# One gate matrix in eight moved to ScalarE, gain rows of the expert layers' end loaded sooner, lead tiles in two banks

## The chip, the cores and the metric

The kernel runs on one core of a Trainium2 chip. A core has TensorE (PE in the profile, with its weight loads as PEld), VectorE (DVE), ScalarE (ACT), GpSimd (POOL) and SyncE (SP), which here only issues transfers; each engine works through its own list of instructions in order. The metric is the device time of one execution in microseconds (us).

## The reference, cut to what matters

Two blocks stand behind each other, each with a mixer (retention and pooling; then a gated recurrence and a state-space scan) and an expert layer. The change touches the two expert layers alone. 512 tokens each pick 128 of 16384 experts, eight heads with 16 each:

```python
s1, i1 = lax.top_k(s[:, :, 0], PEER_TOPK)
s2, i2 = lax.top_k(s[:, :, 1], PEER_TOPK)
cand = s1[..., :, None] + s2[..., None, :]
cidx = i1[..., :, None] * PEER_NKEYS + i2[..., None, :]
best, pos = lax.top_k(cand, PEER_TOPK)
eidx = jnp.take_along_axis(cidx, pos, axis=-1)
g = jax.nn.softmax(best, axis=-1)
act = jax.nn.gelu(jnp.einsum('thkd,td->thk', u[eidx], hb), approximate=False)
out = jnp.einsum('thk,thkd->td', g * act, v[eidx])
```

Behind it stand x = x + g2 * out and a norm with a gain row.

## The kernel before

The class `Peer` does an expert layer, once for each block ("layer 1" and "layer 2" below). For 384 of the 512 tokens it does not gather rows but multiplies with all 16384 experts, 128 at a time (a "tile"), and weights each product with a dense matrix G[expert, token] that holds the gates; the last 128 tokens go the gathering way (`sparse`), between the dense work.

**The gate stage** (end of `early`) builds G. A token's 128 choices are pairs (first, second) of numbers below 128, with a gate each. For eight tokens at a time (an "octet", 48 of them in a layer) `onehots` makes, on DVE, `gb`: 1 where a lane's second number equals the column (one instruction for all eight tokens, L2070), and for each token `ga`: the gate where its first number equals the column, else 0 (eight instructions, L2074). `gbuild` multiplies ga and gb of each token on PE, four tokens to a PSUM bank named `ch` (three such banks), and ACT copies each bank to the staging tile `gst` (L2088), which SP stores when 32 tokens are in it (L2090). `ga` and `gb` have three buffers each; the loop makes octet n+2 before it multiplies octet n. The lists of first, second and gate come from `lists_T`, which transposes them into `hkT`.

Between the octets PE does the products of the first 60 expert tiles with the tokens (`s_quarters`, tiles `mm`): a quarter of a tile per octet, so that four octets ("a cycle") go with one tile: one split of a loaded tile `ur` into high and low parts (`uh` on ACT, L111, `ul` on DVE, L114) and one Gelu (`act`, L2113).

**The lead** (`steady`, first loop) does five more tiles with `s_step`, all in the PSUM bank `p0` (L2254), before the loop over the 128 tiles of the second matrix begins. `s_step` issues a load three tiles ahead, splits the next tile, and then multiplies its own.

**The loop** over i takes each tile's G and activation, loads a tile of `v` two ahead (`vr`, L2275), prepares it (`v_prep`: G times activation, then high and low parts `vh`, `vl`, `wh`, `wl`), and multiplies into eight banks `pv`. `side` slips the gathered rows of the sparse tokens in between. When the 256 gathered rows are done, `ending` calls `done` (in `ffn`), which loads two rows across all partitions: the layer's output gate (`gr<-gate`, L2356) and the gain of the norm (L2357). Then it updates the sparse tokens (`take`, L2368; `update`, L2376 and L2378) in halves between the last tiles.

Of the kernel before, what the change touches and what calls it, by code (L numbers as in the profile page):

```python
# [10 lines left out]
F32 = mybir.dt.float32  # L11
# [4 lines left out]
AF = mybir.ActivationFunctionType  # L16
ALU = mybir.AluOpType
# [1746 lines left out]
class Peer:  # L1764
# [73 lines left out]
    def early(self):  # L1838
        tc, E, P, ps = self.tc, self.E, self.pfx, self.ps
        W0, *pools = self.prev  # L1840
        kp = tc.alloc_tile_pool(name=P + "k", bufs=2, side="right")
# [18 lines left out]
        self.acts = tc.alloc_tile_pool(name=P + "a", bufs=6)  # L1860
        qp = tc.alloc_tile_pool(name=P + "q", bufs=2)
        ws = Weights(E, qp, [(self.wq, 128 * j, 128) for j in range(2, 16)], 2, (self.WLO,))
        self.hkT = kp.tile([128, self.ND, 3, 128], F32, name="hkT", bufs=1)
        self.gf = kp.tile([128, 4, 8, 16], F32, name="gf", bufs=1)
        self.ef = kp.tile([128, 4, 8, 16], F32, name="ef", bufs=1)
        self.at = 1
# [27 lines left out]
        nc, v = self.nc, self.nc.vector  # L1894
# [160 lines left out]
    def lists_T(self, tb, i12):  # L2055
        nc, E = self.nc, self.E
        pt = self.ps.tile([128, 3, 128], F32, name="tp")
        nc.tensor.transpose(pt[:, 0, :], i12[:, 0, :], E.ident)
        nc.tensor.transpose(pt[:, 1, :], i12[:, 1, :], E.ident)
        nc.tensor.transpose(pt[:, 2, :], self.gf[:, tb].rearrange("p h k -> p (h k)"), E.ident)  # L2060
        nc.scalar.activation(self.hkT[:, tb], pt, AF.Copy)

    def onehots(self, n, gp):

        nc, E = self.nc, self.E
        tb, q = divmod(n, 16)
        sh = [128, 8, 128]
        a = gp.tile(sh, F32, name="ga")
        b = gp.tile(sh, F32, name="gb")
        nc.vector.tensor_tensor(b, E.iota[:, None, :].to_broadcast(sh),  # L2070
                                self.hkT[:, tb, 1, q * 8:q * 8 + 8, None].to_broadcast(sh), op=ALU.is_equal)
        for i in range(8):
            first, gate = (self.hkT[:, tb, z, q * 8 + i:q * 8 + i + 1] for z in (0, 2))
            nc.vector.tensor_scalar(a[:, i, :], E.iota, first, gate, op0=ALU.is_equal, op1=ALU.mult)  # L2074
        return a, b

# [70 lines left out]
    def steady(self, vp, psv):  # L2147
        E = self.E
        self.accs = vp.tile([128, 1024], F32, name="accs", bufs=1)
        sps = self.sparse(vp)  # L2150
        next(sps)
        self.pv = [[psv.tile([128, 512], F32, name=f"pv{tb}{dh}") for dh in range(2)] for tb in range(self.ND)]
        done = 0
        for _ in range(self.LEAD):
            self.s_step(self.L0 + done)
            if not done:
                self.v_load(0, vp)
                self.v_load(1, vp)
            done += 1
        self.v_prep(0, vp)  # L2160
        if self.fill is not None:
            E.fill, E.rate = self.fill(vp), 0.4
        owed = 0.0
        full = self.s_by[-1] - self.LEAD + self.S_END + self.VF * (self.SPARSE_END - self.S_END)
        finish = None

        def rows(tail=False):
            return vp.tile([128, 1024], F32, name="vr" if tail else "gr", bufs=3 if tail else self.LAG + 1)

        def ending():  # L2170
            nonlocal finish
            yield from sps
            finish = take, update, squares, factor = self.done(rows)
            src = self.accs[:, :512], self.accs[:, 512:]
            for h in range(2):
                yield
                take(3, src, h)
                update(3, h)
            for h in range(2):
                yield  # L2180
                squares(3, h)
            yield
            factor(3)

        steps = ending()

        def side():
            nonlocal owed
            owed += 256 / full * (1.0 if i < self.S_END else self.VF)
            while owed >= 1 and finish is None:  # L2190
                owed -= 1
                next(steps)
            if finish is not None:
                next(steps, None)

        for i in range(124):
            self.v_load(i + 2 if i < 122 else 128, vp)
            if i == 117 and self.after is not None:
                self.after.preload()
            if i == 119:  # L2200
                self.v_load(124, vp, True)
                self.v_load(125, vp, True)
            elif i in (122, 123):
                self.v_load(i + 4, vp)
            while done < self.s_by[i]:
                self.s_step(self.L0 + done, side)
                done += 1
                E.tick()
            side()
            if i < 123:  # L2210
                self.v_prep(i + 1, vp)
            if i in (121, 122):
                self.v_prep(i + 3, vp, True)
            elif i == 123:
                self.v_prep(126, vp)
            E.tick()
            self.v_mm((i,))
        self.v_prep(127, vp)
        self.acts.release()
        after = self.after  # L2220
        if after is not None:
            after.open()
        E.drain()
        for _ in steps:
            pass
        self.v_mm(range(124, 128))
        take, update, squares, factor = finish

        def add(tb, h):
            update(tb, h)  # L2230
            squares(tb, h)

        later = []
        for tb in range(self.ND):
            for h in range(2):
                if tb == 0 and after is not None:
                    after.weights()
                take(tb, self.pv[tb], h)
                if (tb, h) == (2, 0):
                    factor(1)  # L2240
                if tb == 2 and after is not None:
                    later.append(lambda h=h: add(2, h))
                else:
                    add(tb, h)
                if (tb, h) == (1, 1):
                    factor(0)
        if after is not None:
            after.tail = *later, lambda: factor(2)
        else:
            factor(2)  # L2250

    def s_step(self, e, side=None):
        self.s_load(e + 3)
        pm = self.E.pair.tile([128, self.TD], F32, name="p0")  # L2254
        self.s_split(e + 1, "dve")
        if side:
            side()
        self.s_mm(e, pm, range(8))
        self.s_gelu(e, pm)
# [211 lines left out]
```

## Time and profile before

| | us |
|---|---|
| median of 3 runs | 3571.43 (3567.28 to 3572.85) |
| the profiled execution, own time | 3559.23 |
| its span, first to last instruction | 3557.5 |
| PE busy | 3377.0 (95%) |
| DVE busy | 2827.5 (79%) |
| ACT busy | 1358.8 (38%) |

The shares are means over stages with different limits; the gate stages, from about 911 to 1080 us and from 2542 to 2712 us, and the ends of the expert layers, about 1835 to 1925 us and 3465 to 3557 us, are read by themselves. In a row of the timeline, the number behind an arrow in brackets is the idle time of the engine just before, and what ended it.

### The profile page before, as it was taken

How to read it: one execution, taken by the hardware profiler on the slowest of the kernel's cores; microseconds unless marked ns; L12 is line 12 of the kernel's file. 1: busy time of each engine (PE TensorE's matmuls, PEld its weight loads, DVE VectorE, ACT ScalarE, POOL GpSimd, SP SyncE). 2: the span in 40 equal slices, each digit the busy share in tenths (PEclk: the TensorE clock that was granted, in tenths of full speed). 3: DMA queues.
4: the chain of work that ended last, by engine and by line, in shares of the span. 5: the costliest groups of instructions: out<-in, count | busy, mean ns of one | idle time of the engine just before them, and what ended most of it. 6: DMA issues, size and time to landing. Idle time of an engine off the chain costs nothing.

```text
span 3557.5 us, 50422 instructions
## 1 busy us (share of the span) xinstructions
PE 3377.0 (95%) x18339; PEld 3003.5 (84%) x18339; DVE 2827.5 (79%) x5892; ACT 1358.8 (38%) x1930; POOL 981.1 (28%) x848
## 2 busy tenths in 40 slices
PE   8989889999999999999998898999998999999998
PEld 5878668999888888888886787899987888888886
DVE  6655766898996888888876685788996888888886
ACT  4223324333673333333334324432574333333333
POOL 3212531000002444444431442000000444454440
PEclk9999999999999999999999999999999999999999
DMA  5451664443458999999993222344457999999995
GB/s 193 131 160 57 189 208 122 136 142 127 175 199 323 364 376 344 364 346 363 351 317 101 71 72 91 103 139 141 144 195 261 357 373 356 359 351 347 365 331 188
DMA packets 418745, 830.18 MB, mean 233 GB/s; under 512 B 37948, under 2 KB 249776, under 8 KB 415424
## 3 DMA queue, kind: packets, MB, share of 16 engines
q1 hardware_dynamic: 344320, 558.41, 46.3%
q0 software_dynamic: 74176, 268.55, 20.4%
q8 instruction: 144, 2.36, 0.3%
q14 instruction: 105, 0.86, 0.1%
HBM read 744.52 MB, written 82.33 MB: 232 GB/s over the span
## 4 chain that ended last, share of the span: by engine, by line
PE 72%; DVE 18%; DMA 5%; issue 2%; ACT 2%; SPq 1%; POOL 0%; DVEq 0%; ACTq 0%; POOLq 0%
PE pv L118 9%; PE pv L119 9%; PE pv L120 9%; PE mm L118 8%; PE mm L120 8%; PE mm L119 8%; DVE ga L2074 5%; PE p L120 5%; PE p L118 5%; PE p L119 5%; DVE gb L2070 3%; DMA ada<-in_ada_w_dram 2%; DVE ul L114 1%; DMA ur<-in_peer_u_tiles_dram 1%; DMA x<-in_ada_w_dram 1%
## 5 line engine op out<-in xcount | busy, mean ns | idle before, releaser
L2321 POOL DMA_INDIRECT gr<-in_peer_u_dram,rb x256 | 338.7, 1323 | 1455.0 <-DMA ur<-in_peer_u_tiles_dram 1020.4
L118 PE MATMUL pv<-vh,wh 128*128 128x512 f32 x1512 | 591.1, 391 | 23.6 <-ACT wh L2295 23.6
L119 PE MATMUL pv<-vl,wh 128*128 128x512 f32 x1512 | 590.8, 391 | 0.7 <-DVE vl L2296 0.7
L120 PE MATMUL pv<-vh,wl 128*128 128x512 f32 x1512 | 590.5, 391 | 0.0
L2296 DVE TENSOR_TENSOR vl<-vr,vh 128x1024 fp32r<-128x1024 f32 x252 | 308.6, 1224 | 215.9 <-ACT vh L2294 209.1
L2321 POOL DMA_INDIRECT gr<-in_peer_v_dram,rb x256 | 344.6, 1346 | 389.8 <-DVE accs L2342 331.5
L114 DVE TENSOR_TENSOR ul<-ur,uh 128x1024 fp32r<-128x1024 f32 x256 | 312.7, 1221 | 108.5 <-ACT uh L111 108.4
L118 PE MATMUL p<-hi,uh 128*128 128x384 f32 x1088 | 367.3, 338 | 9.7 <-ACT act L2113 9.7
L120 PE MATMUL p<-hi,ul 128*128 128x384 f32 x1088 | 366.8, 337 | 0.5 <-DVE ul L114 0.5
L2294 ACT ACTIVATE vh<-vr 128x1024 fp32r<-128x1024 f32 x252 | 266.1, 1056 | 264.2 <-issue 224.8
L119 PE MATMUL p<-lo,uh 128*128 128x384 f32 x1088 | 366.3, 337 | 0.0
L118 PEld LDWEIGHTS pv<-vh,wh 128*128 128x128 f32 x1512 | 284.8, 188 | 82.3 <-ACT wh L2295 26.0
L118 PE MATMUL mm<-hi,uh 128*128 128x384 f32 x960 | 334.9, 349 | 3.6 <-ACT qT L1871 3.6
L120 PEld LDWEIGHTS pv<-vh,wl 128*128 128x128 f32 x1512 | 284.4, 188 | 60.7 <-DVE wl L2297 1.5
L2113 ACT ACTIVATE act<-p 128x384 f32<-128x384 f32 x136 | 66.9, 492 | 700.1 <-PE p L120 684.3
L119 PEld LDWEIGHTS pv<-vl,wh 128*128 128x128 f32 x1512 | 284.7, 188 | 57.2 <-DVE vl L2296 2.5
L2342 DVE SCALAR_TENSOR_TENSOR accs<-gr,rb,accs 128x1024 f32<-128x1024 f32 x254 | 325.7, 1282 | 5.4 <-DMA gr<-in_peer_v_dram,rb 0.7
L120 PE MATMUL mm<-hi,ul 128*128 128x384 f32 x960 | 324.5, 338 | 3.9 <-DVE ul L114 3.9
L119 PE MATMUL mm<-lo,uh 128*128 128x384 f32 x960 | 323.7, 337 | 0.0
L2337 DVE SCALAR_TENSOR_TENSOR gr<-gr,hs 128x1024 f32<-128x1024 f32 x256 | 302.9, 1220 | 2.0 <-DMA gr<-in_peer_u_dram,rb 2.0
L111 ACT ACTIVATE uh<-ur 128x1024 fp32r<-128x1024 f32 x256 | 269.0, 1051 | 18.9 <-DMA ur<-in_peer_u_tiles_dram 15.2
L118 PE MATMUL mm<-hi,whi 128*128 128x512 f32 (+1 forms) x656 | 262.7, 400 | 2.8 <-ACT whi L111 1.9
(634 smaller groups left out, 7199.6 us busy)
## 6 DMA issues: line engine op xcount, KB each, us to landing
ur<-in_peer_u_tiles_dram SPq DMA_DIRECT2D x256, 512.0 KB
vr<-in_peer_v_dram SPq DMA_DIRECT2D x252, 512.0 KB
raw<-in_w_in_dram SPq DMA_DIRECT2D x60, 512.0 KB
ada<-in_ada_w_dram SPq DMA_DIRECT2D x96, 256.0 KB
fG<-gst SPq DMA_DIRECT2D x12, 2048.0 KB
f_2G<-gst SPq DMA_DIRECT2D x12, 2048.0 KB
x<-in_ada_w_dram SPq DMA_DIRECT2D x64, 256.0 KB
raw<-in_peer_wq_dram SPq DMA_DIRECT2D x32, 512.0 KB
```

What stands on the lines that cost most here:

```text
L111: nc.scalar.activation(hi, src, AF.Copy)
L114: (nc.vector if e_lo == "dve" else nc.gpsimd).tensor_tensor(lo, src, hi.bitcast(F32), op=ALU.subtract)
L118: nc.tensor.matmul(out, a_hi, b_hi, start=start, stop=False)
L119: nc.tensor.matmul(out, a_hi, b_lo, start=False, stop=False)
L120: nc.tensor.matmul(out, a_lo, b_hi, start=False, stop=stop)
L2070: nc.vector.tensor_tensor(b, E.iota[:, None, :].to_broadcast(sh), self.hkT[:, tb, 1, q * 8:q * 8 + 8, None].to_broadcast(sh), op=ALU.is_equal)
L2074: nc.vector.tensor_scalar(a[:, i, :], E.iota, first, gate, op0=ALU.is_equal, op1=ALU.mult)
L2294: nc.scalar.activation(vh, raw, AF.Copy)
L2296: nc.vector.tensor_tensor(vl, raw, vh.bitcast(F32), op=ALU.subtract)
L2321: nc.gpsimd.indirect_dma_start(out=r, out_offset=None, in_=self.u if n < 128 else self.v, in_offset=bass.IndirectOffsetOnAxis(ap=self.eidx ...
L2337: nc.vector.scalar_tensor_tensor(r, r, 1.0, self.hs, op0=ALU.mult, op1=ALU.mult, accum_out=dots[:, j:j + 1])
L2342: nc.vector.scalar_tensor_tensor(accs, r, w[:, j:j + 1], accs, op0=ALU.mult, op1=ALU.add)
```

## The change

One ga in eight, that of an octet's last token, is made by two instructions on ACT: the distance |first - column|, then max(0, gate - gate * distance), which is the gate at distance 0 and 0 from distance 1 on. For it `hkT` has a fourth list, minus the gate, which DVE makes in `lists_T`. `done` is called behind gathered row 253, two rows sooner, and nothing else of `ending` moves. The five lead tiles take the banks p0 and p1 in turn.

```diff
-        self.hkT = kp.tile([128, self.ND, 3, 128], F32, name="hkT", bufs=1)
+        self.hkT = kp.tile([128, self.ND, 4, 128], F32, name="hkT", bufs=1)
...
-        nc.scalar.activation(self.hkT[:, tb], pt, AF.Copy)
+        nc.scalar.activation(self.hkT[:, tb, 0:3], pt, AF.Copy)
+        nc.vector.tensor_scalar(self.hkT[:, tb, 3], self.hkT[:, tb, 2], -1.0, None, op0=ALU.mult)
...
-            first, gate = (self.hkT[:, tb, z, q * 8 + i:q * 8 + i + 1] for z in (0, 2))
+            first, gate, less = (self.hkT[:, tb, z, q * 8 + i:q * 8 + i + 1] for z in (0, 2, 3))
+            if i == 7:
+
+                nc.scalar.activation(a[:, i, :], E.iota, AF.Abs, scale=-1.0, bias=first)
+                nc.scalar.activation(a[:, i, :], a[:, i, :], AF.Relu, scale=less, bias=gate)
+                continue
             nc.vector.tensor_scalar(a[:, i, :], E.iota, first, gate, op0=ALU.is_equal, op1=ALU.mult)
...
-            yield from sps
-            finish = take, update, squares, factor = self.done(rows)
+            for n, _ in enumerate(sps):
+                if n == 253:
+                    made = self.done(rows)
+                yield
+            finish = take, update, squares, factor = made
...
-        pm = self.E.pair.tile([128, self.TD], F32, name="p0")
+        first = e - self.L0 < self.LEAD
+        pm = self.E.pair.tile([128, self.TD], F32, name=f"p{(e - self.L0) % 2 if first else 0}")
```

On ACT, a cycle of the gate stage of layer 1 before is one Gelu, one split and eight copies of banks:

```order
L2113 ACTIVATE act<-mm 128x384
L2088 ACTIVATE gst<-ch 128x4x128 x2
L111 ACTIVATE uh<-ur 128x1024
L2088 ACTIVATE gst<-ch 128x4x128 x6
L2113 ACTIVATE act<-mm 128x384
```

The same cycle on ACT now:

```order
L2119 ACTIVATE act<-mm 128x384
L2077 ACTIVATE ga<-iota,hkT 128x128
L2078 ACTIVATE ga<-ga,hkT 128x128
L2094 ACTIVATE gst<-ch 128x4x128 x2
L111 ACTIVATE uh<-ur 128x1024
L2077 ACTIVATE ga<-iota,hkT 128x128
L2078 ACTIVATE ga<-ga,hkT 128x128
L2094 ACTIVATE gst<-ch 128x4x128 x2
L2077 ACTIVATE ga<-iota,hkT 128x128
L2078 ACTIVATE ga<-ga,hkT 128x128
L2094 ACTIVATE gst<-ch 128x4x128 x2
```

Behind these rows a fourth pair and its two copies end the cycle. Each pair stands ahead of the copies of the octet two before its own. No table load is added on ACT. On DVE the octets have seven ga each, and three small instructions stand ahead of the first octet:

```order
L114 TENSOR_TENSOR ul<-ur,uh 128x1024
L2062 TENSOR_SCALAR hkT<-hkT 128x128 x3
L2071 TENSOR_TENSOR gb<-iota,hkT 128x1024
L2080 TENSOR_SCALAR ga<-iota,hkT 128x128 x7
L2071 TENSOR_TENSOR gb<-iota,hkT 128x1024
```

Before, a row "ga x8" stood in place of each "ga x7", and no row of L2062. On SP, the transfers of layer 1's end stand before in this order (`hi<-in_w_in_dram` are weights of the next mixer):

```order
L2275 DMA vr<-in_peer_v_dram 128x1024 x4
L152 DMA hi_16768<-in_w_in_dram 128x4x256
L152 DMA hi_16769<-in_w_in_dram 128x4x256
L152 DMA hi_16770<-in_w_in_dram 128x4x256
L152 DMA hi_16771<-in_w_in_dram 128x4x256
L2268 DMA Go<-fG 128x12x128
L2271 DMA old<-fA 128x1536
L2275 DMA vr<-in_peer_v_dram 128x1024 x2
L2268 DMA Go<-fG 128x12x128
L2271 DMA old<-fA 128x1536
L2275 DMA ur<-in_peer_v_dram 128x1024 x2
L2356 DMA gr<-gate_78 128x1024
```

And now:

```order
L2285 DMA vr<-in_peer_v_dram 128x1024 x2
L2366 DMA gr<-gate_78 128x1024
L2367 DMA lo_16761<-in_final_g_dram 128x1024
L2285 DMA vr<-in_peer_v_dram 128x1024 x2
L152 DMA hi_16825<-in_w_in_dram 128x4x256
```

The two rows of the layer's end move ahead of fourteen other transfers of that stretch; layer 2 has the same move, without the four `hi` loads. On ACT, the rows of the lead show the banks (a Gelu reads each tile from its bank), before:

```order
L2113 ACTIVATE act_10250<-p0_10223 128x384
L111 ACTIVATE uh_10163<-ur_10161 128x1024
L2113 ACTIVATE act_10291<-p0_10264 128x384
L111 ACTIVATE uh_10221<-ur_10219 128x1024
L2113 ACTIVATE act_10324<-p0_10297 128x384
```

and now:

```order
L2119 ACTIVATE act_10301<-p0_10274 128x384
L111 ACTIVATE uh_10214<-ur_10212 128x1024
L2119 ACTIVATE act_10342<-p1_10315 128x384
L111 ACTIVATE uh_10272<-ur_10270 128x1024
L2119 ACTIVATE act_10375<-p0_10348 128x384
```

The order on ACT is the same; only the bank alternates. The orders of PE and POOL do not change.

## Rows read from the trace of the kernel before

**Rows 1.** The page's part 4: the chain that ended last, by line.

```profile
PE pv L118 9%; PE pv L119 9%; PE pv L120 9%; PE mm L118 8%; PE mm L120 8%; PE mm L119 8%; DVE ga L2074 5%; PE p L120 5%; PE p L118 5%; PE p L119 5%; DVE gb L2070 3%; DMA ada<-in_ada_w_dram 2%; DVE ul L114 1%; DMA ur<-in_peer_u_tiles_dram 1%; DMA x<-in_ada_w_dram 1%
```

**Rows 2.** Windows: stretch, its length, busy by engine (instructions), clock, DMA; gate stages.

```profile
957.09:1068.19 111.10, 102.42 (x706) 93.68 (x705) 111.10 (x298) 78.39 (x81) 0.00 (x0) 1.00 0.55 204
2546.36:2699.12 152.76, 142.29 (x995) 131.62 (x994) 152.76 (x409) 110.20 (x114) 0.00 (x0) 1.00 0.53 197
```

**Rows 3.** Timeline of DVE in the gate stage of layer 1: start, length, instruction.

```profile
941.99 1.22 DVE L2070 TENSOR_TENSOR gb<-iota,hkT 128x1024 f32<-128x1024 f32 x1
943.12 2.14 DVE L2074 TENSOR_SCALAR ga<-iota,hkT 128x128 f32<-128x128 f32 x8
945.18 1.22 DVE L114 TENSOR_TENSOR ul<-ur,uh 128x1024 fp32r<-128x1024 f32 x1
946.31 1.22 DVE L2070 TENSOR_TENSOR gb<-iota,hkT 128x1024 f32<-128x1024 f32 x1
```

**Rows 4.** Timeline of ACT in the same cycle.

```profile
949.14 2.14 ACT L2088 ACTIVATE gst<-ch 128x512 f32<-128x512 f32 x2 [2.17 <-PE ch L2086]
951.21 0.49 ACT L2113 ACTIVATE act<-mm 128x384 f32<-128x384 f32 x1
952.33 2.15 ACT L2088 ACTIVATE gst<-ch 128x512 f32<-128x512 f32 x2 [0.62 <-PE ch L2086]
954.27 1.06 ACT L111 ACTIVATE uh<-ur 128x1024 fp32r<-128x1024 f32 x1
```

**Rows 5.** Timeline of ACT, two earlier stretches with operands like the new pair's.

```profile
30.36 0.72 ACT L308 ACTIVATE nz<-nz,AB 128x512 f32<-128x512 f32 x1 [5.07 <-DVE nz L305]
31.11 0.63 ACT L309 ACTIVATE hi<-nz 128x512 fp32r<-128x512 f32 x1
...
613.52 0.39 ACT L323 ACTIVATE nl<-nz,AB 128x128 f32<-128x128 f32 x1
```

**Rows 6.** Timeline of DVE where layer 1's gate stage begins.

```profile
909.16 0.23 DVE L2049 TENSOR_SCALAR ei<-ei 128x128 int32<-128x128 int32 x1
909.42 0.23 DVE L2050 TENSOR_SCALAR ei<-ei 128x128 int32<-128x128 int32 x1
```

**Rows 7.** Timeline of PE early in that stage, while it still has a backlog.

```profile
915.99 1.95 PE L2086 MATMUL ch<-ga,gb 128*128 128x128 f32 x16
...
918.81 1.95 PE L2086 MATMUL ch<-ga,gb 128*128 128x128 f32 x16
```

**Rows 8.** Timeline of SP's queue at the end of layer 1.

```profile
1840.49 12.57 SPq L2275 DMA_DIRECT2D vr<-in_peer_v_dram  x4
...
1870.43 0.40 SPq L2356 DMA_DIRECT2D gr<-gate  x1
```

**Rows 9.** Timeline of DVE: the first `take` of layer 1 and of layer 2.

```profile
1879.50 0.69 DVE L2368 TENSOR_TENSOR vr<-accs,gr 128x512 f32<-128x512 f32 x1 [14.08 <-DMA gr<-gate]
...
3509.72 0.69 DVE L2368 TENSOR_TENSOR vr<-accs,gr 128x512 f32<-128x512 f32 x1 [9.20 <-DMA gr<-gate]
```

**Rows 10.** Timeline of PE: where the products go on behind that wait, both layers.

```profile
1882.77 0.79 PE L118 MATMUL pv<-vh,wh 128*128 128x512 f32 x1 [12.07 <-ACT wh L2295]
...
3513.00 0.80 PE L118 MATMUL pv<-vh,wh 128*128 128x512 f32 x1 [7.19 <-ACT wh L2295]
```

**Rows 11.** Timeline of ACT: the next tile's split at layer 1's end.

```profile
1869.83 1.06 ACT L2294 ACTIVATE vh<-vr 128x1024 fp32r<-128x1024 f32 x1 [5.72 <-DMA vr<-in_peer_v_dram]
```

**Rows 12.** Windows, columns as in the second group: ends of both layers, lead of layer 2.

```profile
1850.00:1855.00 5.00, 5.00 (x24) 4.14 (x23) 4.12 (x6) 2.01 (x3) 0.00 (x0) 1.00 0.41 133
...
1885.00:1890.00 5.00, 5.00 (x21) 4.08 (x21) 3.50 (x7) 3.18 (x7) 0.00 (x0) 0.92 0.52 164
...
2740.00:2750.00 10.00, 7.09 (x25) 6.34 (x25) 3.59 (x4) 4.11 (x7) 0.00 (x0) 0.70 0.59 189
...
3515.00:3520.00 5.00, 5.00 (x18) 4.04 (x17) 3.51 (x6) 1.53 (x4) 0.00 (x0) 0.76 0.42 157
```

**Rows 13.** Timeline of PE in the lead: two of layer 1, one of layer 2.

```profile
1096.39 0.44 PE L118 MATMUL p<-hi,uh 128*128 128x384 f32 x1 [0.58 <-ACT act L2113]
...
1109.14 0.45 PE L120 MATMUL p<-hi,ul 128*128 128x384 f32 x1 [0.26 <-DVE ul L114]
...
2740.97 0.69 PE L118 MATMUL p<-hi,uh 128*128 128x384 f32 x1 [3.76 <-ACT act L2113]
```

**Rows 14.** Timeline of ACT in the lead of layer 1: the fifth tile's split.

```profile
1106.77 1.06 ACT L111 ACTIVATE uh<-ur 128x1024 fp32r<-128x1024 f32 x1 [5.42 <-DMA ur<-in_peer_u_tiles_dram]
```

## The prediction

> **What bounds the kernel now.** I read the chain that ended last first, to see where a change could count at all. Most of it is PE, but gb, ga and ul on DVE together hold nine hundredths of the span [rows 1]. Then the busy times by stretch: in both gate stages DVE is busy for the whole of the stretch, to the hundredth, while ACT is busy for 78.39 of 111.10 us and PE for 102.42 [rows 2]. So there DVE sets the pace and ACT has room. The first stretch is eight cycles of 13.89 us. The timeline of DVE shows what such a cycle is made of, by the distance from start to start: gb 1.13, eight ga 2.06 (0.257 each), ul 1.13 [rows 3]. Four octets and one ul are 4 x (1.13 + 2.06) + 1.13 = 13.89, so nothing else is in it. PE's own need I take from where it still works off a backlog: from octet to octet 2.82 us, a quarter of a tile included, 11.3 a cycle [rows 7].
>
> Next I looked for the longest waits at the layers' ends. At the first `take` DVE stands for 14.08 us in layer 1 and 9.20 in layer 2, each time for the transfer of the gate row [rows 9]. DVE is in order, so the preparation of the next tile stands behind it, and PE runs dry: 12.07 and 7.19 us [rows 10]. In SP's queue that row is issued at 1870.43, thirty us behind the four `vr` loads that begin at 1840.49 [rows 8].
>
> The lead I read last. There PE waits 0.58 us for the bank at each tile [rows 13], but the fifth tile's split waits 5.42 us for a load [rows 14], and its product goes on at 1109.14 when ul is there [rows 13].
>
> **Part 1, one ga to ACT.** DVE loses 48 ga of 0.257 in each layer: 12.3 us. It gains three small negations ahead of the first octet; the nearest rows of that shape start 0.26 apart [rows 6], so 0.8, and as DVE never idles there all of it counts. Net 11.5 a layer, 23.1 in both, as long as DVE stays the bound, with a cycle of 4 x (1.13 + 1.80) + 1.13 = 12.86.
>
> Does it? PE needs 11.3, less. ACT is the question. Its cycle now: 78.39 / 8 = 9.80 us as it runs, with pauses between the copies; packed, two copies and what follows take 1.94 when the next reads from SBUF, and with 0.49 for the Gelu and 1.06 for uh [rows 4] that is 4 x 1.94 + 1.55 = 9.3. To this come four pairs. An activation of this size with one column as an operand takes 0.39 [rows 5]. The second of the pair reads what the first wrote; such a pair stands at 30.36 and 31.11, the second 0.03 behind the end of the first (30.36 + 0.72 = 31.08) [rows 5]. The second of ours has two columns, scale and bias, and no row has that: bounds are a whole hiding behind the next instruction (pair 0.42) and twice the one column's 0.39 (pair 0.39 + 0.03 + 0.78 = 1.20). I take it at 0.39, since that row differs by one column only: pair 0.81. Then ACT's cycle is 9.3 + 3.2 = 12.5 packed, 13.0 at today's spacing; at 0.42 it is 11.0 to 11.5, at 1.20 it is 14.1 to 14.6. Against DVE's 12.86 I take the packed one, since a pair stands just where ACT now waits for PE (2.17 and 0.62 in one cycle [rows 4]). The pair of an octet stands two octets ahead of the product that reads it, so PE has no new wait in order.
>
> [...]
>
> **Part 2, the rows sooner.** The gate row now stands behind the second of the four `vr` loads, which are spread over 12.57 us [rows 8], so it is issued near 1845, 25 us sooner, and has 20 us to land before DVE asks at 1879.50 - 14.08 = 1865.4 [rows 9]. Its buffers come free by gathered rows read before; what SP has behind it is `vr`, and those wait for the split of an older tile anyway. The two rows are 1 MB; in 1850 to 1855 the transfer engines are busy for 0.41 of the time [rows 12], so there is room, but bounds are 0 and 1.05 MB / 371 GB/s = 2.8 us (204 GB/s at a share of 0.55 [rows 2]) if they push the next loads. I take 0. What is late next? In layer 1 the split at 1869.83 waits for its own `vr` [rows 11]: vh ends at 1870.9, vl 1.2 later (a ul of that shape [rows 3]), so PE, dry since 1882.77 - 12.07 = 1870.70, goes on at about 1872.1: 1.4 us stay. Layer 2 has no such wait, since the stall there ends with the row alone.
>
> The stall also costs clock. Behind it PE runs at the lower level: in layer 1 from 1882.77 to 1885, and 0.92 granted in the next 5 us; in layer 2 from 3513.0 to 3515, and 0.76 in the next 5 [rows 10, 12]. At half speed that is 1.1 + 0.4 = 1.5 and 1.0 + 1.2 = 2.2. Without the stall it is not lost. Sum: 12.07 - 1.4 + 1.5 = 12.2 in layer 1, 7.19 + 2.2 = 9.4 in layer 2, together 21.6.
>
> **Part 3, two banks.** Four waits of 0.58 go away, and PE is done with the fourth tile some 2 us sooner; but the fifth waits for the load, which hangs on the store of G, not on PE. Gain 0. PE then only stands longer before the fifth tile. In layer 2, where it stood 3.76 us, the clock fell: 0.70 granted over 2740 to 2750, 7.09 us of them busy, so 0.30 x 7.09 = 2.1 us lost [rows 12, 13]. In layer 1 the product behind it takes 0.45 against 0.69 there, so the clock held [rows 13]; with 2 us more of standing I expect the same fall, minus 2.1. Bounds: 0, and 4.2 if layer 2's slow stretch doubles.
>
> **Sum.** 23.1 + 21.6 - 2.1 = 42.6 us. From the profiled execution's own 3559.2 that gives 3516.6; the median of the runs lies 12.2 above that execution, and from it I come to 3528.8, which is what I predict.
>
> **Rivals.** *ACT becomes the bound.* For it: DVE and ACT come within 0.4 us a cycle, and above a pair of 0.89 (packed) or 0.77 (today's spacing) ACT is the longer one. Against: it has 4.1 us free a cycle now. With a cycle of 13.3, midway between 12.5 and 14.1, a layer gains 0.59 x 12 - 0.8 = 6.3, both 12.6, and the time is 3571.4 - (12.6 + 21.6 - 2.1) = 3539.3. [...]
>
> *The end's loads are pushed.* The 1 MB delays what layer 1's next tiles wait for: 2.8 us, 3531.6. Against it the share of 0.41.
>
> *The row isn't there sooner after all*, because SP stands before it longer than I read: Part 2 is then near 0, 3550. Little speaks for it.
>
> *The lead costs nothing*, since the clock holds: 3526.7. The stall lies between a row where it held and one where it fell.
>
> *Slower.* The pair itself: if it keeps ACT for 1.5 us, because a wait of an instruction for the one before it costs more here than at 31.11, ACT's cycle is 9.8 + 6.0 = 15.8, each layer loses 1.9 x 12 + 0.8 = 23.6, and the time is 3571.4 + 47.2 - 19.5 = 3599. It decides from 1.21 us on, where ACT's cycle of 14.64 eats Parts 2 and 3. That is the upper bound of the rows, three times one activation.
>
> **How the numbers follow.** The likeliest, DVE still the bound and the rows in time, has 0.52; ACT as the bound 0.25; pushed loads 0.08; a lead without loss 0.10; rows not sooner 0.03; slower 0.02. The runs of before spread by about 4 us to either side. The first case and the third and fourth fill 3519 to 3536, and the milder part of the ACT case reaches 3545; I leave out what lies beyond. 0.2% (7 us) is about what a measurement can tell from no change: faster 0.96, the same 0.02, slower 0.02.
>
> **What would show it.** Part 1: cycles of 12.9 us with DVE still without idle time, ga at 48 x 7, and a pair on ACT near 0.8; wrong if DVE waits for PE and ACT is full. Part 2: no wait of the first `take`, PE idle of about 1.4 us at layer 1's end and none at layer 2's, full clock behind. Part 3: no wait for the bank, the same landing of the fifth tile's load, and a lower clock behind it in both layers. The forecast is wrong if the pair takes over 0.9, if the ends' loads come late, or if a stage behind the gate stage starts at the time it did before.

## The result, and the profile after

The changed kernel takes 3532.27 us (median of four runs, 3529.46 to 3534.59) against 3572.14 before: a ratio of 0.9891, 95% interval 0.9874 to 0.9908, or 39.9 us less where 42.6 were forecast. The interval reaches from 33 to 45 us less, so the time by itself doesn't tell the two apart; the traces have to. The page of the changed kernel gives span and chain, which answer to [rows 1].

```profile
span 3527.7 us, 50621 instructions
...
PE pv L119 9%; PE pv L118 9%; PE pv L120 9%; PE mm L118 8%; PE mm L120 8%; PE mm L119 8%; PE p L120 5%; PE p L118 5%; PE p L119 5%; PE ch L2092 4%; DMA ada<-in_ada_w_dram 2%; ACT gst L2094 2%; DMA x<-in_ada_w_dram 1%; DMA ur<-in_peer_u_tiles_dram 1%; PE ch L1951 1%
```

ga and gb, eight hundredths of the chain before, are gone from it; ch on PE and gst on ACT stand there instead. In the gate stage three engines are now nearly level (PE busy for 103.33, ACT for 103.61 and DVE for 111.10 of 111.10 us, in the windows below), and the chain took whichever came last.

PE issues the same 18339 products in the same order in both kernels, so the start of one product can be compared between two traces. The table gives the us from one such product to another, by stage, for every kernel of this study (products that a kernel has on top of these are not counted); the products are those that start at 904.49, 1084.91 and 1135.74 (gate stage and lead of layer 1), 1845.15 and 1939.40 (its end), 2536.29, 2714.09 and 2767.72, and 3488.64 and 3548.78 (the same of layer 2) in the trace before. In the changed kernel the ten are at 910.41, 1079.41, 1135.35, 1844.76, 1929.58, 2526.58, 2692.70, 2747.34, 3468.26 and 3519.00.

| kernel | gate 1 | lead 1 | end 1 | gate 2 | lead 2 | end 2 |
|---|---|---|---|---|---|---|
| before | 180.42 | 50.83 | 94.25 | 177.81 | 53.62 | 60.13 |
| changed | 169.00 | 55.94 | 84.81 | 166.12 | 54.64 | 50.74 |
| e1_gate_only | 169.00 | 54.65 | 95.15 | 166.13 | 52.46 | 59.67 |
| e2_rows_only | 180.41 | 53.69 | 84.76 | 177.82 | 53.57 | 50.50 |
| e3_banks_only | 180.43 | 54.23 | 94.44 | 177.78 | 53.81 | 59.85 |
| e12_no_banks | 169.01 | 54.70 | 85.09 | 166.23 | 53.98 | 50.55 |
| two_on_act | 191.57 | 53.65 | 84.73 | 188.11 | 52.80 | 51.13 |
| relu_only | 169.03 | 55.53 | 84.80 | 166.41 | 54.73 | 50.72 |
| hold_clock | 169.00 | 59.09 | 84.29 | 166.30 | 58.81 | 51.56 |
| take_apart | 169.00 | 55.77 | 84.81 | 166.12 | 54.01 | 50.77 |
| weights_later | 168.95 | 54.66 | 80.82 | 166.08 | 53.69 | 51.97 |
| hold_own_bank | 168.97 | 52.23 | 83.83 | 166.07 | 51.14 | 51.02 |
| five_in_32 | 166.22 | 55.71 | 84.75 | 163.25 | 53.74 | 50.53 |
| all_together | 166.27 | 51.96 | 80.50 | 163.57 | 51.13 | 53.57 |

How far these numbers can be trusted is seen in stages that don't differ between two kernels. Gate stages agree to 0.1 us in layer 1 and 0.4 in layer 2. The ends of layer 1 with the rows sooner, and the next stage's weights where they were, agree to 1.3. The leads of layer 2 with one bank spread over 1.5 us, and its ends with the rows sooner over 3.

The stages of the changed kernel give 11.4 - 5.1 + 9.4 + 11.7 - 1.0 + 9.4 = 35.8 us. The spans differ by only 29.8, because the profiled execution of before reached the first product at 904.49 and this one at 910.41, ahead of anything that was changed.

The windows of the stretch of [rows 2] in the changed kernel: DVE still without a pause, ACT at 103.61 of 111.10 where it had 78.39.

```profile
957.09:1068.19 111.10, 103.33 (x758) 99.62 (x757) 111.10 (x287) 103.61 (x155) 0.00 (x0) 1.00 0.61 224
```

The timeline of DVE in that stage, beside [rows 3].

```profile
1000.59 1.27 DVE L114 TENSOR_TENSOR ul<-ur,uh 128x1024 fp32r<-128x1024 f32 x1
1001.72 1.27 DVE L2071 TENSOR_TENSOR gb<-iota,hkT 128x1024 f32<-128x1024 f32 x1
1002.86 1.94 DVE L2080 TENSOR_SCALAR ga<-iota,hkT 128x128 f32<-128x128 f32 x7
1004.65 1.28 DVE L2071 TENSOR_TENSOR gb<-iota,hkT 128x1024 f32<-128x1024 f32 x1
...
1013.44 1.28 DVE L114 TENSOR_TENSOR ul<-ur,uh 128x1024 fp32r<-128x1024 f32 x1
```

From ul to ul it is 12.85 us, seven ga taking 1.79 from start to start. ACT in the same cycle, beside [rows 4]:

```profile
1004.60 2.11 ACT L2094 ACTIVATE gst<-ch 128x512 f32<-128x512 f32 x2 [0.70 <-PE ch L2092]
1006.64 0.49 ACT L2119 ACTIVATE act<-mm 128x384 f32<-128x384 f32 x1
1007.03 0.39 ACT L2077 ACTIVATE ga<-iota,hkT 128x128 f32<-128x128 f32 x1
1007.45 0.49 ACT L2078 ACTIVATE ga<-ga,hkT 128x128 f32<-128x128 f32 x1
1007.85 2.01 ACT L2094 ACTIVATE gst<-ch 128x512 f32<-128x512 f32 x2
```

The pair takes 1007.85 - 1007.03 = 0.82 us, 0.42 for the distance and 0.40 for the maximum, which has two columns: it runs for 0.49, and the next one starts 0.09 ahead of its end. The forecast had 0.81, an estimate from the 0.39 of a row with one column [rows 5].

PE in that cycle waits once for ACT's matrix:

```profile
1003.40 2.16 PE L2092 MATMUL ch<-ga,gb 128*128 128x128 f32 x16 [0.86 <-ACT ga L2077]
```

At the layers' ends the timeline of the changed kernel answers to [rows 8 to 11]; SP, ACT, DVE and PE in layer 1, and the first `take` of layer 2:

```profile
1844.81 0.33 SPq L2366 DMA_DIRECT2D gr<-gate  x1
...
1864.94 0.69 DVE L2378 TENSOR_TENSOR vr<-accs,gr 128x512 f32<-128x512 f32 x1
...
1869.44 1.06 ACT L2304 ACTIVATE vh<-vr 128x1024 fp32r<-128x1024 f32 x1 [5.73 <-DMA vr<-in_peer_v_dram]
...
1870.97 0.51 PE L118 MATMUL pv<-vh,wh 128*128 128x512 f32 x1 [0.66 <-ACT wh L2305]
1871.81 0.50 PE L119 MATMUL pv<-vl,wh 128*128 128x512 f32 x1 [0.34 <-DVE vl L2306]
...
1879.12 1.06 ACT L2304 ACTIVATE vh<-vr 128x1024 fp32r<-128x1024 f32 x1 [2.38 <-DMA vr<-in_peer_v_dram]
...
1880.65 0.50 PE L118 MATMUL pv<-vh,wh 128*128 128x512 f32 x1 [0.30 <-ACT wh L2305]
...
3480.05 0.69 DVE L2378 TENSOR_TENSOR vr<-accs,gr 128x512 f32<-128x512 f32 x1
```

Neither `take` waits. PE stands 1.0 us in layer 1 instead of 12.07, and the granted clock behind it is 1.00 in each window of 5 us up to 1895; in layer 2 it is 1.00 from 3480 to 3520. The first tile's split waits for its load as it did [rows 11], and starts 24.68 us behind the mark of the end in both kernels. But now a later split stands 2.38 us for its load, and PE again some tenths at each of the three tiles behind the first. Counted from start to start, the products of these three tiles lose 3.8 us against their usual step of 0.23, where before one tile, at 1903.19, lost 1.1.

The lead of layer 1, beside [rows 13, 14], ACT and PE:

```profile
1102.73 1.06 ACT L111 ACTIVATE uh<-ur 128x1024 fp32r<-128x1024 f32 x1 [8.53 <-DMA ur<-in_peer_u_tiles_dram]
...
1103.84 0.69 PE L118 MATMUL p<-hi,uh 128*128 128x384 f32 x1 [6.01 <-ACT uh L111]
1105.10 0.69 PE L120 MATMUL p<-hi,ul 128*128 128x384 f32 x1 [0.25 <-DVE ul L114]
```

The waits for the bank are gone, PE stands 6.01 us for the load, and then runs at the lower level (0.69 us for its first product, and 0.50 granted in 1105 to 1110). Windows, columns as in [rows 2]:

```profile
1100.00:1105.00 5.00, 1.01 (x2) 0.50 (x2) 1.18 (x1) 2.27 (x3) 0.00 (x0) 0.54 0.64 253
1105.00:1110.00 5.00, 4.90 (x15) 4.90 (x16) 1.74 (x3) 0.11 (x1) 0.00 (x0) 0.50 0.73 247
```

### The profile page after: what moved, and what is told of

The parts are those of the page before. It is cut to its first block, busy times and chain, and to the rows that moved or that the text cites. A ratio compares the mean times of both kernels' runs of the same rounds, so it can differ in the third digit from the quotient of the medians.

```text
span 3527.7 us, 50621 instructions
## 1 busy us (share of the span) xinstructions
PE 3363.1 (95%) x18339; PEld 3002.0 (85%) x18339; DVE 2801.3 (79%) x5802; ACT 1413.1 (40%) x2122; POOL 980.2 (28%) x848
## 4 chain that ended last, share of the span: by engine, by line
PE 77%; DVE 10%; DMA 5%; ACT 5%; issue 2%; SPq 1%; POOL 1%; DVEq 0%; ACTq 0%; POOLq 0%
PE pv L119 9%; PE pv L118 9%; PE pv L120 9%; PE mm L118 8%; PE mm L120 8%; PE mm L119 8%; PE p L120 5%; PE p L118 5%; PE p L119 5%; PE ch L2092 4%; DMA ada<-in_ada_w_dram 2%; ACT gst L2094 2%; DMA x<-in_ada_w_dram 1%; DMA ur<-in_peer_u_tiles_dram 1%; PE ch L1951 1%
```

## The experiments

### One part at a time

Four kernels: each part of the change alone (the other two as before), and the first two without the third. The edit of the last, against the changed kernel:

```diff
-        first = e - self.L0 < self.LEAD
-        pm = self.E.pair.tile([128, self.TD], F32, name=f"p{(e - self.L0) % 2 if first else 0}")
+        pm = self.E.pair.tile([128, self.TD], F32, name="p0")
```

> The kernel before with Part 1 alone (one gate matrix in eight on ACT; rows and banks as before). Theory A (the forecast's sum): both gate stages lose 11.5 us and all of it reaches the end, 3571.4 - 23.1 = 3548.3. Theory B (the lead gives part of it back): in the trace of the changed kernel layer 1's lead starts 5.5 us sooner against the kernel before, but its fifth tile's load lets the split begin only 4.0 us sooner, and PE's clock falls behind the longer wait, so that the steady part starts 0.4 us sooner; there the lead took 5.1 us in layer 1 and 1.0 in layer 2. If that follows from the earlier stage and not from the second bank, this run shows it too: about 3571.4 - 23.3 + 6.1 = 3554.

Measured: 3544.39 us, ratio 0.9931 (0.9917 to 0.9944), some 25 us. The gate stages are those of the changed kernel to 0.01 us. The time is theory A's. Layer 1's lead is 3.8 us longer than in the trace of before though it has one bank, as theory B had it; layer 2's is 1.2 shorter, against it. The next run shows that most of those 3.8 us are not the change's.

> The kernel before with Part 2 alone (the two rows sooner). Theory A (the forecast's sum): 12.2 us in layer 1 and 9.4 in layer 2, 3571.4 - 21.6 = 3549.8. Theory B (the stall hid the next tiles' loads): layer 1 keeps only 9.4 of it, as in the trace of the changed kernel, where PE goes on 11.8 us sooner and then loses 2.3 of that on splits that wait for their loads; both layers 18.8, 3552.6. In the trace: no wait of the first take, and PE idle again for some tenths of a us at each of the next three tiles of layer 1.

Measured: 3546.35 us, ratio 0.9935 (0.9921 to 0.9949), some 23 us. Ends of 84.76 and 50.50, so 9.5 and 9.6 us: theory B, by the trace; the time would allow either. Its lead of layer 1, in which nothing is changed and ahead of which nothing is either, takes 53.69 us, 2.9 more than in the trace before. The kernel is the same up to there, so the 50.83 of before belongs to that execution: the load of the fifth tile let PE go on 1.3 us sooner than here (behind 2.43 us of standing, 3.76 here), and the clock held (1.00 granted from 1105 to 1115; here 0.80 from 1110 to 1115).

> The kernel before with Part 3 alone (two banks for the lead's tiles). Theory A (the forecast): the four waits of 0.58 go, the fifth tile's load lands when it did, PE stands longer and the clock falls behind it, so a loss of 2 us in layer 1 and of 0 to 2 in layer 2: 3571.4 + 2 to + 4, and a granted clock below 0.9 in the 10 us after the fifth tile's start in layer 1. Theory B (banks are worth what they take away): a gain of 2.3 us a layer, 3566.8. Theory C: no difference, the clock in layer 1 holds at 1.00.

Measured: 3569.62 us, ratio 1.0002 (0.9993 to 1.0011): no difference. Leads of 54.23 and 53.81, against 53.69 and 53.57 with one bank: half a us and a quarter longer. The banks bring nothing, and the loss is below what was forecast. The time is theory C's, but its reason is not: in layer 1 the fifth tile's first product takes 0.69 us (its row is shown with the next run) and 0.57 is granted from 1115 to 1120, so the clock did fall.

> The changed kernel without Part 3: one bank for the lead's tiles again, gate matrix and rows as changed. Theory A (the second bank causes the loss of the lead): layer 1's lead gives back less than 5.1 us; PE waits 2.3 us less ahead of the fifth tile and the clock holds, 2 to 4 us faster than the changed kernel, 3528 to 3530. Theory B (the loss comes from the earlier gate stage, whatever the banks): PE stands for about 3.9 us ahead of the fifth tile, as long as layer 2 did in the kernel before, and the clock falls all the same; the same as the changed kernel within 1 us, 3532.

Measured: 3528.24 us, ratio 0.9886 (0.9871 to 0.9901). The interval overlaps with that of the changed kernel, so the times don't decide; the traces do. The fifth tile's first product, timeline of PE in layer 1, of e1_gate_only, e2_rows_only, e3_banks_only and e12_no_banks in this order:

```profile
1101.55 0.69 PE L118 MATMUL p<-hi,uh 128*128 128x384 f32 x1 [3.68 <-ACT act L2119]
```

```profile
1111.77 0.44 PE L118 MATMUL p<-hi,uh 128*128 128x384 f32 x1 [3.76 <-ACT act L2113]
```

```profile
1114.28 0.69 PE L118 MATMUL p<-hi,uh 128*128 128x384 f32 x1 [6.33 <-ACT uh L111]
```

```profile
1100.18 0.69 PE L118 MATMUL p<-hi,uh 128*128 128x384 f32 x1 [3.73 <-ACT act L2119]
```

With one bank PE stands 3.7 us, with or without the new gate stage; the 2.43 of before is the exception. With two it stands 6.0 to 6.3. The tile starts no sooner for it: its first product comes 24.4 to 24.7 us behind the mark of the lead in these four and in the changed kernel, when its load is there (23.35 in the trace of before). What the second bank adds is standing, and the lower level lasts longer behind it: the fifth tile's products come 0.32 us apart until 6.5 us behind the first of them in the changed kernel and 3.2 in e12_no_banks, and 0.17 apart from then on. From the tile's first product to the first pv product it is 9.81 us in the one and 7.91 in the other, each with 1.94 us of standing ahead of that product. The windows of e12_no_banks, whose fifth tile starts at 1100.18; the changed kernel, whose fifth starts at 1103.84, had 0.54 and 0.50 in them:

```profile
1100.00:1105.00 5.00, 4.82 (x19) 4.43 (x20) 2.70 (x3) 1.08 (x2) 0.00 (x0) 0.67 0.55 195
1105.00:1110.00 5.00, 2.71 (x12) 1.72 (x11) 2.34 (x3) 2.80 (x4) 0.00 (x0) 1.00 0.68 182
```

So both theories hold a part. The second bank costs 55.94 - 54.70 = 1.2 us in layer 1, and the other kernels with the earlier gate stage agree (54.65 and 54.66 with one bank, 55.53 to 55.77 with two). In layer 2 the same difference is 0.7, but there leads with one bank reach from 52.46 to 53.98 and with two from 52.80 to 54.73, so that a cost isn't shown. Most of the 5.1 us of layer 1's lead is there without the bank.

### How near ACT is to the bound

```diff
-            if i == 7:
+            if i >= 6:
```

> The changed kernel with two gate matrices in eight on ACT. Theory A (the forecast's: DVE sets the pace at one in eight, and ACT, at 12.5 of 12.86 us a cycle, is full): DVE's cycle falls to 4 x (1.13 + 1.54) + 1.13 = 11.8, but ACT's rises to 9.3 + 8 x 0.81 = 15.8 and takes over; 2.9 us more for each of 12 cycles in two layers, about 70 us slower than the changed kernel, 3602. Rival (ACT's work hides in its waits, and PE's 11.3 is next): a cycle of 11.8, 25 us faster, 3507.

Measured: 3573.57 us, ratio 1.0019 (1.0008 to 1.0029). The gate stages are 22.6 and 22.0 us longer than in the changed kernel, together 45 where theory A had 70; the rival, a gain, is out. ACT is the bound: it has no pause in a cycle, and DVE now waits once a cycle for uh (DVE's timeline),

```profile
1012.56 1.23 DVE L114 TENSOR_TENSOR ul<-ur,uh 128x1024 fp32r<-128x1024 f32 x1 [2.88 <-ACT uh L111]
...
1027.35 1.22 DVE L114 TENSOR_TENSOR ul<-ur,uh 128x1024 fp32r<-128x1024 f32 x1 [2.87 <-ACT uh L111]
```

and the cycle is 14.79 us, not 15.8. Less eight pairs of 0.80 that leaves 8.4 for the rest of ACT's work where the forecast took 9.3. With four pairs ACT needs 8.4 + 3.2 = 11.6, so it has 1.2 us free in 12.86.

```diff
-                nc.scalar.activation(a[:, i, :], E.iota, AF.Abs, scale=-1.0, bias=first)
-                nc.scalar.activation(a[:, i, :], a[:, i, :], AF.Relu, scale=less, bias=gate)
+                nc.scalar.activation(a[:, i, :], E.iota, AF.Relu, scale=less, bias=gate)
```

> The changed kernel with the second of the pair alone on ACT: the distance is left out, so that the eighth gate matrix has wrong values; everything else runs as in the changed kernel, with 0.42 us less on ACT for an octet. Theory A (DVE is the bound of the gate stages): the same time as the changed kernel within 2 us, 3532, DVE still busy all the time and cycles of 12.87. Rival (ACT is the bound or shares in it): up to 4 x 0.42 = 1.7 us less a cycle, until PE's 11.3 or DVE's own pace stops it; a gain of some us.

Measured: 3528.03 us, ratio 0.9887 (0.9872 to 0.9902), gate stages of 169.03 and 166.41 where the changed kernel has 169.00 and 166.12. This kernel leaves out the distance. Half of the pair less on ACT, and nothing gained: DVE is the bound.

```diff
-            if i == 7:
+            if i == 7 or i == 6 and n % 4 == 3:
```

> The changed kernel with one more gate matrix on ACT in every fourth octet (five of 32 instead of four). By the run with two in eight ACT's own cycle is 14.79 us with eight pairs, so 11.6 with four and 12.4 with five; DVE's is 12.87 - 0.26 = 12.61. Theory A (DVE is the bound and ACT has 1.2 us free a cycle): cycles of 12.6, 24 x 0.26 = 6.2 us faster than the changed kernel, 3526. Rival (ACT can't use its free time, since it stands 0.7 us a cycle for PE's products at a fixed place and PE stands 0.86 for ACT's matrix): no gain, 3532, or a loss.

Measured: 3522.28 us, ratio 0.9877 (0.9860 to 0.9893). DVE goes from one ul to the next in 12.61 us (timeline):

```profile
1011.36 1.21 DVE L114 TENSOR_TENSOR ul<-ur,uh 128x1024 fp32r<-128x1024 f32 x1
...
1023.97 1.21 DVE L114 TENSOR_TENSOR ul<-ur,uh 128x1024 fp32r<-128x1024 f32 x1
```

The gate stages are 2.8 and 2.9 us shorter than in the changed kernel: theory A, by the traces; the intervals of the two times overlap.

### What the end of layer 1 waits for next

```diff
-                bufs[tb] = (spare(2), spare(3)) if out is None and tb == 2 else (alloc(True), alloc())
+                bufs[tb] = (spare(2), spare(3)) if out is None and tb == 2 else (alloc(tb < 3), alloc())
```

> The changed kernel with the product of the end's first `take` in a buffer of the gathered rows instead of one of the three vr buffers. In the changed kernel that buffer is held from 1864.94 until ACT's square of 1883.59, and PE waits 0.30 and 0.35 for splits at 1880 to 1882 and again at 1886 and 1893, 2.4 us in all with the clock. Theory A (the vr buffer is missing to the loads of the next tiles): loads are issued some us sooner, the wait of 2.38 ahead of the split of 1879.12 goes, and layer 1's end gains 1 to 2.4 us; layer 2, where no such wait stands, nothing: 3530 to 3531. Rival (transfers are late by the rate of the memory, not by the buffer): no change, 3532.

Measured: 3530.62 us, ratio 0.9897 (0.9882 to 0.9912); the end takes 84.81 us, as in the changed kernel to the hundredth. The split waits as long as before, with the transfer engines full ahead of it (ACT's timeline, and a window):

```profile
1876.23 1.06 ACT L2304 ACTIVATE vh<-vr 128x1024 fp32r<-128x1024 f32 x1 [2.44 <-DMA vr<-in_peer_v_dram]
```

```profile
1870.00:1875.00 5.00, 5.00 (x24) 4.01 (x23) 3.83 (x6) 1.86 (x5) 0.00 (x0) 1.00 1.01 405
```

By their distance from the mark of the end, the loads that stand at 1871.79 in the changed kernel were issued 2.4 us sooner, and nothing came of it. The buffer isn't what is missing. The rival stands.

```diff
-            if i == 117 and self.after is not None:
+            if i == 121 and self.after is not None:
                 self.after.preload()
```

This kernel also has the lead's tiles in one bank, so that e12_no_banks is what it is compared with.

> The changed kernel without Part 3 (3528.2 in its run), and the four weight loads of the next stage (`hi`, 0.5 MB each) moved from step 117 to step 121 of layer 1's end. Theory A (the rate of the transfers is what is late next there: the transfer engines are busy without a gap from 1855 to 1875, and with another buffer loads were issued 2.3 us sooner and nothing was gained): the 2 MB are 5.4 us at 371 GB/s, the vr and old loads behind them land sooner, the waits of 0.66, 0.34, 0.30, 0.35, 0.34 and 0.58 of PE shrink, and layer 1's end gains 1 to 2.8 us: 3525.5 to 3527. Rival (the weights are then late for the next stage, whose first split starts at 1894.60): a loss of up to 5 us there, 3533.

Measured: 3521.80 us, ratio 0.9873 (0.9856 to 0.9889). The end takes 80.82 us, 4.3 less than in e12_no_banks, more than theory A gave, and all_together below has the gain again (80.50). The intervals of the two times overlap; the gain stands on the traces. Of PE's waits up to 1900 one is left (its timeline):

```profile
1887.01 0.50 PE L118 MATMUL pv<-vh,wh 128*128 128x512 f32 x1 [0.27 <-ACT wh L2304]
```

The splits wait for PE's reads now, not for loads (ACT's timeline), and the next stage isn't late.

```profile
1872.51 1.06 ACT L2303 ACTIVATE vh<-vr 128x1024 fp32r<-128x1024 f32 x1 [0.76 <-PE pv L120]
```

### What the clock costs in the lead

```diff
         if side:
             side()
+        if e == self.L0 + 4:
+            pd = self.E.pair.tile([128, self.TD], F32, name="p1")
+            for _ in range(32):
+                self.nc.tensor.matmul(pd, self.hhi[:, 0, :128], self.hhi[:, 0, :self.TD], start=True, stop=True)
         self.s_mm(e, pm, range(8))
```

> The changed kernel with 32 more products of 384 columns (5.5 us at full clock, into the lead's idle second bank, read by nothing) between the fourth and the fifth tile of the lead in both layers. Theory A (the loss of the lead is PE's clock, which fell behind 6.01 and 4.67 us of standing): the fifth tile's 24 products run at 0.17 us a step instead of 0.32, which took 2.6 us in layer 1, and the first pv products follow at full clock, 1.1 us more there and 1.5 in layer 2; about 5 us faster than the changed kernel, 3527. Rival (the later landing of the fifth tile's load is all of it): no gain, 3532, or a loss of 1 us a layer, where the added products reach past the landing.

Measured: 3536.64 us, ratio 0.9915 (0.9902 to 0.9929), the leads 3.2 and 4.2 us longer. I had read the order wrong: the fourth tile's Gelu stands behind the fifth tile's split on ACT, so its bank isn't idle at all. The added products began after the wait, at the lower level (0.55 granted from 1100 to 1105; PE):

```profile
1100.09 7.85 PE L2271 MATMUL p<-hi 128*128 128x384 f32 x32 [4.90 <-ACT act L2119]
```

That run says nothing on the clock. The next has 26 products, into `pm`, the fifth tile's own bank.

> The changed kernel with 26 more products of 384 columns (4.5 us at full clock, read by nothing) between the fourth and the fifth tile of the lead, this time in the fifth tile's own bank, which is free as soon as the third tile's Gelu is done. In the run with the other bank they waited 4.90 us for the fourth tile's Gelu, so that they came behind the wait and not into it. Theory A (the clock is what the lead loses): PE does not stand, the fifth tile's first product takes 0.44 or less instead of 0.69, granted clock 1.00 until the pv products; 3 to 5 us faster than the changed kernel, 3528. Rival (the pv products' wait of 1.94 lowers the clock anyway, and the added ones reach past the load's landing): 3531 to 3533.

Measured: 3519.15 us, ratio 0.9871 (0.9851 to 0.9891). PE works through most of the wait, and the fifth tile runs at a granted clock of 1.00 (timeline of PE and ACT, and a window):

```profile
1098.40 4.69 PE L2270 MATMUL p<-hi 128*128 128x384 f32 x26
...
1103.46 1.06 ACT L111 ACTIVATE uh<-ur 128x1024 fp32r<-128x1024 f32 x1 [8.53 <-DMA ur<-in_peer_u_tiles_dram]
...
1104.57 0.45 PE L118 MATMUL p<-hi,uh 128*128 128x384 f32 x1 [1.47 <-ACT uh L111]
```

```profile
1100.00:1110.00 10.00, 7.80 (x42) 6.84 (x40) 2.92 (x3) 2.43 (x4) 0.00 (x0) 1.00 0.69 264
```

The leads are 3.7 and 3.5 us shorter than in the changed kernel, and 2.5 and 2.8 shorter than in e12_no_banks: theory A. The load has no part in it: the split waits 8.53 us as in the changed kernel, and in both layers the fifth tile's first product comes at the same distance from the mark of the lead to 0.1 us (24.4 in layer 1). But from there to the first pv product it is 7.28 us instead of 9.81. Useless work in a wait that wasn't shortened was worth 7.2 us in the two leads. The same products with one bank were not run, so whether the second bank has a share in the gain is not shown.

### All that gained

> The changed kernel with all three: weight loads at step 121, 26 products ahead of the fifth tile, five of 32 on ACT. Theory A: the gains lie in different stages and add up, 3532.3 - (1 to 2.8) - (3 to 5) - 6.2 = 3519 to 3522. Rival (one of them gains nothing, as its own run beside this one shows): the sum of the others.

Measured: 3515.99 us, ratio 0.9858 (0.9838 to 0.9877), the fastest by its median; its interval still touches those of the three single edits. By the table the gains of gate stages, leads and layer 1's end are all there, but layer 2's end takes 53.57 us, 2.8 more than in the changed kernel. Windows give a granted clock of 0.93 in 3480 to 3490 and 0.90 in the 10 us behind it; with PE busy for 9.22 and 10.00 us there that is about 1.7 of the 2.8 us. Why it falls there I haven't found.

## Why the prediction held, and where its sum was off

**Part 1** was right in mechanism and size: 11.5 us a layer forecast, 11.4 and 11.7 measured; a cycle of 12.86 forecast, 12.85 measured; the pair 0.81 against 0.82. ACT wasn't as near to being the bound as the forecast had it, which came from packing its cycle to 9.3 us where 8.4 is possible. The prediction's "PE has no new wait in order" was wrong: PE waits 0.86 a cycle for ACT's matrix, which costs nothing while DVE sets the pace. e1_gate_only has this part's gain at some 25 us, with slower work on an engine that had time: 0.82 us for the pair on ACT where a ga takes 0.257 on DVE [rows 3].

**Part 2** was right for layer 2 (9.4 forecast, 9.4 measured) and too high for layer 1 (12.2 against 9.4). The step that failed is the answer to "What is late next?": it looked at the first tile's split alone, and put the loads of the tiles behind it at nothing. That there was room was read from a share of 0.41 in 1850 to 1855. That window was the lull ahead of the four weight loads; from 1855 to 1875 the transfer engines are full (shares of 1.07, 1.16, 1.04 and 1.09 in windows of 5 us). Two of these windows of before, with the columns of [rows 12] (a transfer counts whole where it starts, so a share can pass 1):

```profile
1855.00:1860.00 5.00, 5.00 (x24) 4.14 (x23) 2.52 (x4) 2.40 (x4) 0.00 (x0) 1.00 1.07 357
...
1870.00:1875.00 5.00, 0.70 (x4) 0.24 (x2) 0.00 (x0) 0.88 (x1) 0.00 (x0) 1.00 1.09 369
```

Before, DVE's stall covered these late loads; without it the three tiles behind the first cost 2.7 us more. weights_later shows what they compete with: 4.3 us come back when the next stage's weights go last. That the missing 2.8 us equal the bound of the prediction for the moved 1 MB is chance as far as the traces go: the first tile's split, whose load stands behind those rows, waits 5.73 us where it waited 5.72, and layer 2, with the same rows moved and no weight loads, lost nothing. A run without the 1 MB, which would settle it for the later tiles, was not made. The wait left at the first tile was 1.0 us instead of 1.4. The half speed that the sum of this part takes behind the stalls is in the trace of before: 0.50 granted from 1882.77 to 1885 and from 3513 to 3515.

**Part 3**: loss instead of gain was right: 2.1 us were forecast, all in layer 1, and the second bank costs 1.2 there (0.5 in e3_banks_only); layer 2's 0.7 lies within the spread. That the time of e3_banks_only shows none of it is within what a median can tell. Wrong was the ground under it: "in layer 1 the clock held" was true of one execution. In three other traces with one bank PE stands 3.68 to 3.76 us there and the clock falls (0.83 granted from 1095 to 1105 in e1_gate_only and in e12_no_banks, 0.80 from 1110 to 1115 in e2_rows_only), so by e2_rows_only 2.9 of the 5.1 us by which the lead grew between the two profiles are no effect of the change. The second bank didn't make a clock fall that held; with it the lower level lasted longer (6.5 us against 3.2). So the size came out near by luck.

With 53.69 us for the lead of before, the stages give 38.7 us, close to the 39.9 of the medians. The forecast's 42.6 less the 2.8 of layer 1's end is 39.8; that this meets the medians to 0.1 us is chance, with an interval of 12 us around them.

Of the rivals, ACT as the bound is out by relu_only. Loads were late in layer 1, as the second had it, but that the moved rows pushed them isn't shown. Rows not sooner is out, with the gate row issued at 1844.81. The lead without loss is out by the traces of layer 1, if by little more than 1 us, and the slower case, a pair of over 1.21 us, is out too.

## What to carry to other kernels

Move work to the engine with free time even if it is slower there (0.82 against 0.257 us here), and find its limit with one run that moves too much: the packed cycle of that run says how much more fits. When a long stall is taken away, look at the transfers that landed in its shadow over the whole stretch that follows, not in one lull; a load for the next stage can be moved behind them. A wait for a transfer in one profile is one draw (PE stood 2.43 us in one trace and 3.68 to 3.76 in three others); compare it with the same wait in another layer, or run the kernel again, before a clock that held is counted on.

## What the runs showed of the hardware

A wait of PE that the kernel doesn't shorten was filled: with 4.69 us of products that nobody reads in it the granted clock was 1.00 from 1100 to 1110, and the tile behind it began with a product of 0.45 rather than 0.69 us (hold_own_bank). Behind waits of nearly the same length the clock fell at different moments: behind 3.76 us the first product still took 0.44 (e2_rows_only, whose clock then was 0.80 on average over 1110 to 1115), behind 3.68 (e1_gate_only) and 3.73 (e12_no_banks) it took 0.69. And in the changed kernel a second ACT instruction that reads the result of the first, with two columns as operands, started 0.42 us behind the first's start, which itself takes 0.39: there was no wait beyond these 0.03 us.
